# A convolution's output product in pairs of rows: seven half products, sums on GpSimd, the gate kept in DRAM

## The chip, the cores and the metric

The kernel runs on one core of a Trainium2 chip. The metric is the device time of one execution in microseconds (us). The median of three runs of the kernel before is 1639.84 us (1639.81 to 1642.17).

## What is computed

One layer of a backbone with D = 1024 channels, on 128 context tokens and 512 latent tokens, 640 in all, in float32: a gated feed-forward step, a mixer, a second feed-forward step, a final norm. The change lies in the mixer, in the branch of the short convolution and what follows it:

```python
def mixer(h, ...):
    z = h @ w_in + b_in
    ...
    ml = (o * hm) @ w_ml_out
    bg = z[..., B_OFF:C_OFF]
    cg = z[..., C_OFF:X_OFF]
    xs = z[..., X_OFF:GML_OFF]
    u = cg * xs
    ...                                   # uc = centred width-3 convolution of u along the tokens
    sc = (bg * uc) @ w_sc_out             # 1024 x 1024: the product that the change rewrites
    y = jax.nn.sigmoid(z[..., GML_OFF:GSC_OFF]) * ml + jax.nn.sigmoid(z[..., GSC_OFF:IN_COLS]) * sc
    return y @ w_o, C, n, m
...
    mod = jax.nn.silu(cond) @ w_mod + b_mod          # nine vectors of 1024: shifts, scales, gates
    sh1, sc1, g1, shm, scm, gm, sh2, sc2, g2 = jnp.split(mod, N_MOD, axis=-1)
    ...
    x = x + gm[:, None, :] * y
    h = modulate(rmsnorm(x, norm_g[2]), sh2, sc2)
```

## The kernel before, in words

Channels lie on the 128 partitions and tokens along the free axis, so that a row (an output block of 128 channels) is 128 x 640, in two halves of 320 tokens. A float32 product is made of three passes of TensorE (`three`, L288 to L290): weight and activation are each split into a rounded high part and a residual (`split`: ScalarE casts the high part, L75, VectorE subtracts it, L79, named wh/wl for weights, ...h/...l for activations), and hi x hi, hi x lo and lo x hi are added up in PSUM. Each pass is one matmul of 128 x 128 weights on 320 tokens.

A plain row (`plain_el`) is 8 blocks of input channels x 2 halves x 3 passes = 48 matmuls. It consumes two weight operands of 128 x 512, each cast and subtracted once.

A pair (`pair_el`) computes two rows at once. Seen as 2 x 2 blocks (two rows by two halves of the input channels, times two halves of the input channels by two halves of the tokens) it needs seven block products instead of eight, 12 matmuls each, 84 in all, in the order A11, S1, S2, A12, S3, S4, A22. Seven weight operands are split, of which four (S1 to S4) are sums made first (`ws`, L270); S1 and S3 are made on GpSimd where the pair is built with `G`, the rest on VectorE. The activations have seven block operands as well ("11", "21", "22" and the sums "T1" to "T4"). The partial results are moved between PSUM banks by ScalarE (L332, L343, L347) and VectorE: L360 adds the stored S1 product to the bank in which A22 is accumulated next, so A22 waits for L360, and S4's product runs in between. With `spare_v` a ScalarE copy (L357) reads that bank in place of L360. L367 makes the first row's second half. Then `ev` is called for each of the four quarters.

Each engine works through its instructions in the order in which the code emits them. Weight operands are cast four ahead of their use, evictions come after the product that they read, and what `lazy` holds (splits of activations, side terms of the convolution) is emitted in portions between the products. `fill` spreads other steps over the products of an element.

The stages around the change, in the order of the kernel before:
- The convolution's inputs: pairs `cx_pair` (u and its convolution, into the tiles CV) and `bg_pair` (times bg, then split into Bh/Bl), both with sums on GpSimd.
- The gate: four pairs `gsc_pair` (sigmoid, kept in SBUF as GS), sums on VectorE.
- The convolution's output product: eight plain rows over `w_sc_out`; `sc_ev` multiplies by the gate (L2078), adds the other branch's row t, which `t_in` loads back from DRAM (td), halved on the way (L2079), and splits the result into YB.
- The output projection: rows over `w_o`, five plain ones and three in `halves_el`, added into the residual X (L1020), which `x_in` loads back; then the squares for the next norm (L883).
- Modulation vectors: a half of one (512 channels) is computed either on TensorE (`mod_half`: two bursts of four matmuls, L649, and four transposes, L661) or on VectorE (`mod_dve`: 16 instructions of 128 x 512, or 32 of 128 x 256, L767 and L769, then four small matmuls, L778, and two transposes, L786). Three halves are done on VectorE between the rows of `w_sc_out` and `w_o`: both of SC2 and one of G2, in halves of 256 (`h_wide`).

## Time and profile before

| | |
|---|---|
| profiled execution: time | 1639.97 us |
| its span | 1637.9 us |
| TensorE busy | 1616.8 us (99%) |
| VectorE busy | 1308.5 us (80%) |
| ScalarE busy | 883.4 us (54%) |
| GpSimd busy | 318.6 us (19%) |
| convolution's inputs, gate, output product | about 890 to 1037, 1037 to 1083, 1083 to 1140 us of the span |

Times inside the span are counted from its start. A row of a timeline gives start, duration, engine, line, operation, output <- inputs and shape; consecutive instructions overlap a little, so what an instruction costs its engine is the distance from its start to the next one's. A row of a table of windows gives, for a stretch, its length and then each engine's busy time, with the number of instructions in brackets. A row of a table of groups gives the count, the busy time, the mean duration in ns, and the idle time before them.

### The profile page before, as it was taken

Reading aid. Unit: us, or ns where it says so; the run is one execution under the profiler, and the core shown is the slowest. Engines: PE = TensorE matmul, PEld = TensorE weight load, DVE = VectorE, ACT = ScalarE, POOL = GpSimd, SP = SyncE. Lnnn points to the kernel's source line nnn. Section 1 sums busy time; section 2 is a strip of 40 time slices with the busy share of each in tenths; the row PEclk is TensorE's granted clock in tenths of the full one; section 3 lists DMA queues with packets and bytes.
Section 4 is the critical chain, followed back from the end, with each engine's and each line's share of the span. In section 5 each row is a group of like instructions: output and inputs, shape, how many; then the busy total and the mean of one; then the engine's idle time right before and its main releaser. Section 6 shows DMA issues by size and latency. Waiting matters only on the chain.

```text
span 1637.9 us, 29686 instructions
## 1 busy us (share of the span) xinstructions
PE 1616.8 (99%) x10997; PEld 1570.5 (96%) x10997; DVE 1308.5 (80%) x2738; ACT 883.4 (54%) x1957; POOL 318.6 (19%) x441
## 2 busy tenths in 40 slices
PE   8999999999999999999999999999999999999998
PEld 5999999999989999999999999999999999999997
DVE  6878878979777878878887899779688877786765
ACT  5556555655376646555561455533275665565543
POOL 2312311120121322111022222011123113113002
PEclk9999999999999999999999999999999999999999
DMA  9897966785552534333367433357377768468432
GB/s 322 223 228 176 229 134 136 185 224 161 151 180 75 121 90 111 80 94 76 89 215 244 114 91 103 109 174 220 117 187 186 149 133 196 104 137 195 135 114 64
DMA packets 334225, 248.69 MB, mean 152 GB/s; under 512 B 11764, under 2 KB 306043, under 8 KB 334081
## 3 DMA queue, kind: packets, MB, share of 16 engines
q1 hardware_dynamic: 280560, 174.09, 36.8%
q0 software_dynamic: 53488, 72.70, 21.1%
q8 instruction: 86, 1.41, 0.4%
q14 instruction: 59, 0.48, 0.1%
q10 hardware_dynamic: 32, 0.01, 0.0%
HBM read 210.48 MB, written 36.28 MB: 151 GB/s over the span
## 4 chain that ended last, share of the span: by engine, by line
PE 85%; DVE 8%; ACT 3%; issue 1%; DMA 1%; SPq 1%; ACTq 0%; DVEq 0%
PE ps L288 26%; PE ps L289 26%; PE ps L290 26%; DVE wl L79 2%; PE ax L1799 2%; PE ax L1830 2%; DMA wr<-in_ffn_w_dram 1%; PE ax L1802 1%; DVE ws L270 1%; ACT wh L75 1%; PE ax L1776 1%; DVE ma L769 0%; ACT Uh L934 0%; SPq L627 0%; DVE Uh L926 0%
## 5 line engine op out<-in xcount | busy, mean ns | idle before, releaser
L79 DVE TENSOR_TENSOR wl<-wr,wh 128x512 fp32r<-128x512 f32 (+1 forms) x397 | 279.0, 712 | 86.5 <-ACT wh L75 84.4
L79 DVE TENSOR_TENSOR wl<-ws,wh 128x512 fp32r<-128x512 f32 x308 | 211.5, 687 | 62.1 <-ACT wh L75 61.6
L75 ACT CAST wh<-wr 128x512 fp32r<-128x512 f32 (+1 forms) x399 | 235.5, 606 | 35.5 <-PE ps L289 13.4
L75 ACT CAST wh<-ws 128x512 fp32r<-128x512 f32 x308 | 189.2, 620 | 96.8 <-DVE ws L270 86.3
L288 PE MATMUL ps<-HT4h,wh 128*128 128x320 f32 x440 | 138.9, 316 | 1.0 <-DVE t L360 0.9
L288 PE MATMUL ps<-Uh,wh 128*128 128x320 f32 x440 | 137.2, 312 | 0.0
L289 PE MATMUL ps<-HT4l,wh 128*128 128x320 f32 x440 | 136.5, 310 | 0.6 <-DVE HT4l L79 0.5
L289 PE MATMUL ps<-Ul,wh 128*128 128x320 f32 x440 | 136.0, 309 | 0.0
L290 PE MATMUL ps<-HT4h,wl 128*128 128x320 f32 x440 | 136.0, 309 | 0.0
L290 PE MATMUL ps<-Uh,wl 128*128 128x320 f32 x440 | 135.7, 308 | 0.0
L288 PE MATMUL ps<-HT3h,wh 128*128 128x320 f32 x388 | 122.0, 314 | 1.0 <-ACT ps L347 0.8
L289 PE MATMUL ps<-HT3l,wh 128*128 128x320 f32 x388 | 119.9, 309 | 0.0
L290 PE MATMUL ps<-HT3h,wl 128*128 128x320 f32 x388 | 119.9, 309 | 0.0
L288 PE MATMUL ps<-H11h,wh 128*128 128x320 f32 x376 | 119.1, 317 | 0.5 <-ACT H11h L75 0.5
L288 PE MATMUL ps<-H21h,wh 128*128 128x320 f32 x376 | 117.5, 312 | 0.0
L289 PE MATMUL ps<-H11l,wh 128*128 128x320 f32 x376 | 116.5, 310 | 0.7 <-DVE H11l L79 0.4
L290 PE MATMUL ps<-H21h,wl 128*128 128x320 f32 x376 | 116.2, 309 | 0.0
L290 PE MATMUL ps<-H11h,wl 128*128 128x320 f32 x376 | 116.2, 309 | 0.0
L289 PE MATMUL ps<-H21l,wh 128*128 128x320 f32 x376 | 116.0, 309 | 0.0
L235 POOL DMA_DIRECT2D wr<-in_ffn_w_dram x48 | 62.2, 1454 | 275.3 <-DMA wr<-in_ffn_w_dram 121.4
L288 PE MATMUL ps<-H22h,wh 128*128 128x320 f32 x344 | 107.9, 314 | 0.0
L289 PE MATMUL ps<-H22l,wh 128*128 128x320 f32 x344 | 106.5, 310 | 0.4
(489 smaller groups left out, 4929.7 us busy)
## 6 DMA issues: line engine op xcount, KB each, us to landing
wr<-in_ffn_w_dram SPq DMA_DIRECT2D x94, 512.0 KB, 5.8
wr<-in_w_in_dram SPq DMA_DIRECT2D x72, 512.0 KB, 3.9
wr<-in_w_mod_dram SPq DMA_DIRECT2D x59, 512.0 KB, 4.1
xd<-x POOLq DMA_DIRECT2D x56, 320.0 KB, 6.8
wr<-in_ffn_w_dram SPq DMA_DIRECT2D x52, 256.0 KB, 4.4
wr<-in_ffn_w_dram POOLq DMA_DIRECT2D x48, 256.0 KB, 5.3
early<-in_w_mod_dram SPq DMA_DIRECT2D x13, 512.0 KB, 8.8
wq<-in_ffn_w_dram SPq DMA_DIRECT2D x24, 256.0 KB, 3.1
```

What stands on the lines that cost most here:

```text
L75: A.copy(hi, raw)
L79: V.tensor_sub(lo, raw, f32(hi))
L235: queue.dma_start(t[:, 512 * o:512 * o + 512].rearrange("p (k n) -> p k n", k=4), dap(w, (row0 + 512 * half) * ncol + col0, [[ncol, P], [P ...
L270: engine.tensor_add(t, part(o, a), part(o, b))
L288: PE.matmul(ps, hi[:, ws], ah, start=start, stop=False, skip_group_check=True)
L289: PE.matmul(ps, hi[:, ws], al, start=False, stop=False, skip_group_check=True)
L290: PE.matmul(ps, lo[:, ws], ah, start=False, stop=stop, skip_group_check=True)
L1776: PE.matmul(p[:, :P], S["k", dt][:, sl], S["q", dt][:, sl], start=(dt == 0), stop=(dt == 1))
L1799: PE.matmul(p2[:, :DH + 1], S["q", dt][:, sl], S["C"][d][:, dt, :], start=(dt == 0), stop=(dt == 1))
L1802: PE.matmul(p1[:, :DH + 1], S["p", ch][:, d, :], PO["vt"][:, ch, :], start=True, stop=True)
L1830: PE.matmul(p[:, :DH + 1], kw[:, dt * P:(dt + 1) * P], PO["vt"][:, ch, :], start=True, stop=True)
```

## The change

The eight plain rows over `w_sc_out` become four pairs (`sc_pair`). Their seven activation operands per block of input channels are made in `bg_pair` and after it: "11", "T1", "21" and "22" in the B pool (`own`), "T2", "T3" and "T4" in tiles that the layer's input gives free (`lent`). The sums for T1 to T4 are 16 instructions of 128 x 320 on GpSimd. The gate's pairs make their S1 and S3 on GpSimd too; two of them run before the convolution's inputs, two after. Their sigmoids are written to DRAM (sd), and `rows_in` loads gate and other branch back two rows at a time. The halving of the other branch is moved into the constant `HM`, so that the addition (L2098 of the new kernel) is a plain sum, on GpSimd for the second half of the tokens. One half of SC2 is computed on TensorE (`own_units`, in the second and third pair), the other half and G2's on VectorE beside the rows of `w_o`, in one piece of 512. Five rows of `w_o` have the residual of their weights subtracted on GpSimd (`lo=G`).

```diff
+    SO = {o: [None] * 4 for o in OPS_H}
+    LENT = {"T2": "11", "T3": "T1", "T4": "T2"}
...
     def bg_pair(m):
         def ev(mi, h, src):
-            uc = CV[m + mi][:, hsl(h)]
-            V.scalar_tensor_tensor(uc, src, bias(B_OFF + (m + mi) * P), uc, op0=OP.add, op1=OP.mult)
-
-            def put_b():
-                PB[m + mi, h] = bpair()
-                split(uc, *PB[m + mi, h])
-            lazy.append(put_b)
+            r, k = m + mi, (m + mi) % 4
+            c0, c1 = (CV[k][:, hsl(i)] for i in range(2))
+            d0, d1 = (CV[r][:, hsl(i)] for i in range(2))
+            uc = (d0, d1)[h]
+            V.scalar_tensor_tensor(uc, src, bias(B_OFF + r * P), uc, op0=OP.add, op1=OP.mult)
+            if h == 0:
+                lazy.append(own("11" if r < 4 else "21", k, d0))
+            elif r < 4:
+                lazy.extend([lambda: G.tensor_sub(c0, c1, c0), own("T1", k, c0)])
+            else:
+                lazy.extend([own("22", k, d1), lambda: G.tensor_sub(c0, c0, d1), lambda: G.tensor_sub(c1, c1, d1),
+                             lambda: G.tensor_add(d0, d0, c0)])
...
     def gsc_pair(m):
         def ev(mi, h, src):
-            if h == 0:
-                GS[m + mi] = xp.tile([P, T], F32, name="x", bufs=KT)
-            A.activation(GS[m + mi][:, hsl(h)], src, AF.Sigmoid, bias=bias(GSC_OFF + (m + mi) * P))
+            t = t3()
+            A.activation(t, src, AF.Sigmoid, bias=bias(GSC_OFF + (m + mi) * P))
+            G.dma_start(sd[m + mi][:, hsl(h)], t)
...
-    def sc_ev(m):
-        def ev(h, ps):
-            g = GS[m][:, hsl(h)]
-            t = TL[m, h]
-            V.tensor_mul(g, ps, g)
-            V.scalar_tensor_tensor(t, t, 0.5, g, op0=OP.mult, op1=OP.add)
...
+    def rows_in(m):
+        for i in range(m, m + 2):
+            for to, src in ((GS, sd), (TL, td)):
+                to[i] = xp.tile([P, T], F32, name="x", bufs=KT)
+                G.dma_start(to[i], src[i])
...
+    def sc_pair(m):
+        def ev(mi, h, src):
+            r = m + mi
+            g = GS[r][:, hsl(h)]
+            V.tensor_mul(g, src, g)
+            (G if h else V).tensor_add(g, g, TL[r][:, hsl(h)])
...
+    def own_units(pairs, ch, half, p0):
+
+        us, fs = mod_half(ch, half, True)
...
-        conv.append(pair_el(*bg_pair(m), G, spare_v=True))
-    conv += weave([pair_el(*gsc_pair(m)) for m in range(0, KT, 2)], [step(lambda: None)] * 3 + [step(t_in(0))])
-    prog += with_units(conv, mod_dve(SH2, (0,), m_wide), places=[1, 0, 0] * 3 + [1] + [0] * 4)
...
-    sc = [plain_el(w_load(w_sc_out, 0, KT, m * P, D), KT, lambda k, h: PB[k, h], sc_ev(m)) for m in range(KT)]
...
-    prog += with_units(sc + wo, mod_dve(SC2, (0, 1), h_wide) + mod_dve(G2, (1,), h_wide), 2)
+    conv = gs[:2] + cx[:2] + bg[:1] + cx[2:4] + bg[1:2] + cx[4:] + bg[2:] + gs[2:]
+    prog += with_units(conv, mod_dve(SH2, (0,), m_wide), places=[1, 1, 0, 1, 1] + [0] * 9)
...
+    sc = []
     for m in range(0, KT, 2):
...
+        at = {6: [lambda m=m: rows_in(m + 2)]} if m < 6 else {5: [relax, lambda: [x_in(k) for k in range(4)]]}
...
+        sc.append(pair_el(*sc_pair(m), G, acts=SO, at=at))
+    own_units(sc, SC2, 0, 1)
...
+    wo = [dict(el, ops=[dict(o, lo=G) for o in el["ops"]]) for el in wo]
...
+    prog += sc + with_units(wo, mod_dve(SC2, (1,), ma_wide) + g2, places=[2, 2, 1, 2, 1])
```

What VectorE has to do in the output product is other work afterwards. In the kernel before, its instructions for one plain row, from the gate's multiplication of the first half to the last split of a weight, and the first of the modulation's instructions that follow (ps is PSUM, x the gate's tile, t3 the other branch's, wr a loaded weight; the numbers name buffers):

```order
L2078 TENSOR_TENSOR x_13277<-ps_13787,x_13277 128x320
L2079 SCALAR_TENSOR_TENSOR t3_13703<-t3_13703,x_13277 128x320
L2078 TENSOR_TENSOR x_13277<-ps_13788,x_13277 128x320
L2079 SCALAR_TENSOR_TENSOR t3_13705<-t3_13705,x_13277 128x320
L79 TENSOR_TENSOR H11l_13866<-t3_13703,H11h_13865 128x320
L79 TENSOR_TENSOR HT3l_13870<-t3_13705,HT3h_13869 128x320
L79 TENSOR_TENSOR wl_13878<-wr_13857,wh_13877 128x512
L79 TENSOR_TENSOR wl_13882<-wr_13857,wh_13881 128x512
L769 SCALAR_TENSOR_TENSOR HT1h_13713<-wr_13743,cm_93,HT1h_13713 128x256
```

In the changed kernel, VectorE's instructions from the second pair's A12 product on, to the end of that pair:

```order
L2097 TENSOR_TENSOR x_13931<-ps_13939,x_13931 128x320
L2098 TENSOR_TENSOR x_13931<-x_13931,x_13933 128x320
L270 TENSOR_TENSOR ws_14025<-ws_14005,wr_13830 128x512
L79 TENSOR_TENSOR wl_14028<-ws_14005,wh_14027 128x512
L360 TENSOR_TENSOR t3_14043<-ps_14003,t3_13983 128x320
L79 TENSOR_TENSOR H21l_14046<-x_13744,H21h_14045 128x320
L79 TENSOR_TENSOR wl_14059<-ws_14025,wh_14058 128x512
L367 TENSOR_TENSOR t3_13983<-ps_13958,t3_13983 128x320
L2097 TENSOR_TENSOR x_13931<-t3_13983,x_13931 128x320
L79 TENSOR_TENSOR H22l_14078<-x_13744,H22h_14077 128x320
L79 TENSOR_TENSOR H21l_14082<-x_13931,H21h_14081 128x320
L79 TENSOR_TENSOR wl_14088<-wr_13830,wh_14087 128x512
```

The modulation's instructions have gone from here, and sums and splits of weights have come, with L360 in their middle. GpSimd has only loads at this place in the kernel before (t3 from td, x from the residual's xd):

```order
L2091 DMA x_13873<-xd_133 128x640
L2069 DMA t3_13897<-td_174 128x320
L2069 DMA t3_13899<-td_174 128x320
L2091 DMA x_13961<-xd_133 128x640
L2069 DMA t3_13985<-td_174 128x320
```

In the changed kernel it has, from the first pair's end into the second (ws a sum of weights, x the gate's and the other branch's tiles):

```order
L2098 TENSOR_TENSOR x_13740<-x_13740,x_13742 128x320
L270 TENSOR_TENSOR ws_13909<-wr_13469,wr_13615 128x512
L2089 DMA x_13931<-sd_182 128x640
L2089 DMA x_13933<-td_174 128x640
L2089 DMA x_13935<-sd_182 128x640
L2089 DMA x_13937<-td_174 128x640
L2098 TENSOR_TENSOR x_13744<-x_13744,x_13746 128x320
L270 TENSOR_TENSOR ws_14005<-wr_13969 128x512
```

Sums of activations and of weights now share GpSimd's queue with the loads of the next two rows. On TensorE the modulation's four matmuls stand between the S3 and S4 products of the second pair and of the third:

```order
L290 MATMUL ps<-HT1h,wl 128x320
L649 MATMUL ax<-wr,cm 32x512 x4
L288 MATMUL ps<-Bh,wh 128x320
```

They come ahead of S4 there, and so between L360's input and the product A22 that waits for L360.

More of the change, by code (lines that the diff above doesn't have):

```diff
@@ L72, in mixer_step, with split @@
     owed = []
-    def split(raw, hi, lo, owe=False):
+    def split(raw, hi, lo, owe=False, engine=None):
         A.copy(hi, raw)
@@ L78, in split @@
         else:
-            V.tensor_sub(lo, raw, f32(hi))
+            (engine or V).tensor_sub(lo, raw, f32(hi))
     RAWB, HALFB, OPB, SB, AHEAD = 5, 1, 6, 3, 4
@@ L2216, in mixer_step @@
                     {0: (), 1: (3, 2, 1), 2: (2, 2, 2), 3: (3, 2)})
-    els[0][0][0]["fill"] = [step(f) for f in N["later"] + [lambda: None] * 6]
+    els[0][0][0]["fill"] = [step(f) for f in N["later"] + g2_end + [lambda: None] * 6]
+    els[0][0][0]["first"] = []
+    els[0][0][1]["first"] = [lambda: PO["ma_x"].close()]
     els[0][0][-1]["fill"] = [step(half_gate(G2))]
```

80 lines of the change are left out of this document (51 added, 29 removed).

## The prediction

> **What bounds the kernel now.** I read the busy times of the page first, then a table of windows over the stages that the change touches, then TensorE's waits there. In the windows the columns after the length are TensorE, its weight loads, VectorE, ScalarE and GpSimd; then come TensorE's granted clock, the DMA share and GB/s.
>
> ```profile
> PE 1616.8 (99%) x10997; PEld 1570.5 (96%) x10997; DVE 1308.5 (80%) x2738; ACT 883.4 (54%) x1957; POOL 318.6 (19%) x441
> ...
> 890.00:940.00 50.00, 50.00 (x347) 49.38 (x347) 43.64 (x72) 21.25 (x43) 13.52 (x12) 1.00 0.45 130
> 940.00:990.00 50.00, 49.48 (x334) 48.80 (x334) 46.75 (x79) 27.38 (x56) 11.79 (x8) 1.00 0.32 87
> 990.00:1037.00 47.00, 45.84 (x308) 44.89 (x307) 44.43 (x82) 25.09 (x52) 6.02 (x4) 1.00 0.37 100
> 1037.00:1086.00 49.00, 49.00 (x339) 48.39 (x338) 32.18 (x57) 28.66 (x58) 3.25 (x6) 1.00 0.44 127
> 1086.00:1114.00 28.00, 28.00 (x196) 27.39 (x195) 27.26 (x66) 6.71 (x14) 4.77 (x9) 1.00 0.74 222
> 1143.00:1178.00 35.00, 35.00 (x245) 34.38 (x244) 25.86 (x60) 10.70 (x24) 4.96 (x6) 1.00 0.49 145
> ...
> PE ps L288 <- DVE t L360: 0.9, 2, 0.5
> ```
>
> TensorE is the bound everywhere, at full clock: in the output product (1086 to 1114) and the gate (1037 to 1086) it never stops. So a matmul taken away shows in the time, unless another engine takes over. The candidate is VectorE: 44.43 us of 47 in the convolution's inputs, where pairs with sums on GpSimd run as they will in the output product, and there TensorE does lose 0.52 and 1.16 us (50 - 49.48, 47 - 45.84). 0.9 us of that waits for L360, the eviction that must be done before a pair's last product. So VectorE near 95% costs TensorE 1 to 2.5%: what the change is worth hangs on VectorE in the new pairs.
>
> **TensorE: 48 matmuls fewer.** Eight plain rows have 8 x 48 = 384 matmuls, four pairs 4 x 84 = 336. One costs the distance between starts, not its duration of 0.31 us:
>
> ```profile
> 1083.11 0.31 PE L288 MATMUL ps<-Bh,wh 128*128 128x320 f32 x1
> ...
> 1091.03 0.31 PE L288 MATMUL ps<-Bh,wh 128*128 128x320 f32 x1
> ```
>
> These two have 53 matmuls between them: 7.92 / 54 = 0.1467 us. 48 of them are 7.04 us. A pair is 84 x 0.1467 = 12.32 us, a product 1.76 us.
>
> **TensorE: a half of a modulation comes to it.** Two bursts of four matmuls and four transposes; the first feed-forward has the same, here one burst and one set of transposes with their neighbours:
>
> ```profile
> 125.83 0.30 PE L290 MATMUL ps<-HT3h,wl 128*128 128x320 f32 x1
> 126.06 1.06 PE L649 MATMUL ax<-wr,cm 128*32 128x512 f32 x8
> ...
> 127.31 0.31 PE L289 MATMUL ps<-H22l,wh 128*128 128x320 f32 x1
> ...
> 139.34 0.31 PE L290 MATMUL ps<-HT3h,wl 128*128 128x320 f32 x1
> 139.49 0.60 PE L661 MATMUL ax<-ident,t 128*128 128x128 f32 x4
> ...
> 140.08 0.30 PE L289 MATMUL ps<-H22l,wh 128*128 128x320 f32 x1
> ```
>
> The outer rows are two ordinary steps apart (0.29 us) where nothing stands between them. So a burst costs 127.31 - 125.83 - 0.29 = 1.19 us, the transposes 140.08 - 139.34 - 0.29 = 0.45; in all 2 x 1.19 + 0.45 = 2.83 us. What the half cost TensorE while VectorE made it, four small matmuls and two transposes, goes:
>
> ```profile
> 1110.24 0.31 PE L290 MATMUL ps<-Bh,wl 128*128 128x320 f32 x1
> ...
> 1111.30 0.30 PE L289 MATMUL ps<-Bl,wh 128*128 128x320 f32 x1
> ...
> 1118.04 0.31 PE L290 MATMUL ps<-Bh,wl 128*128 128x320 f32 x1
> ...
> 1118.55 0.31 PE L289 MATMUL ps<-Bl,wh 128*128 128x320 f32 x1
> ```
>
> In the same way (1.06 - 0.29) + (0.51 - 0.29) = 0.99 us. Net +1.84 us. The two halves that stay on VectorE cost TensorE what they did. TensorE's own sum is -7.04 + 1.84 = -5.2 us.
>
> **VectorE in the new pairs.** Its price per instruction is again a distance between starts:
>
> ```profile
> 957.53 0.48 DVE L79 TENSOR_TENSOR Bl<-x,Bh 128x320 fp32r<-128x320 f32 x1
> 957.93 0.69 DVE L79 TENSOR_TENSOR wl<-wr,wh 128x512 fp32r<-128x512 f32 x1
> 958.53 0.48 DVE L79 TENSOR_TENSOR Bl<-x,Bh 128x320 fp32r<-128x320 f32 x1
> ```
>
> 0.40 us for 320 columns, 0.60 for 512. By the order, the four pairs hold 31 instructions of 512 and 45 of 320 (seven weight splits, two sums, four products with the gate, two additions, four splits, L360 and L367 a pair, two lent operands extra, and less at the end where GpSimd splits `w_o`): 18.6 + 18.0 = 36.6 us, and I add 2 us for three small ones of the modulation and for instructions that read the result of the one before. On top comes what GpSimd takes from VectorE:
>
> ```profile
> 946.17 0.74 DVE L769 SCALAR_TENSOR_TENSOR x<-wr,cm,x 128x512 f32<-128x512 f32 x1
> ...
> 947.76 1.78 DVE L769 SCALAR_TENSOR_TENSOR x<-wr,cm,x 128x512 f32<-128x512 f32 x1
> ...
> 947.64 1.34 POOL L270 TENSOR_TENSOR ws<-wr 128x512 f32<-128x512 f32 x1 [1.75 <-issue]
> ...
> L79 DVE TENSOR_TENSOR wl<-wr,wh 128x512 fp32r<-128x512 f32 x35 | 31.0, 892 | 5.2 <-ACT wh L75 5.0
> L79 DVE TENSOR_TENSOR wl<-ws,wh 128x512 fp32r<-128x512 f32 x43 | 29.3, 682 | 1.2 <-ACT wh L75 1.2
> L769 DVE SCALAR_TENSOR_TENSOR x<-wr,cm,x 128x512 f32<-128x512 f32 x28 | 23.7, 857 | 0.3
> L1943 DVE SCALAR_TENSOR_TENSOR t<-t,biT,t 128x320 f32<-128x320 f32 x6 | 6.2, 1028 | 0.0
> L2046 DVE SCALAR_TENSOR_TENSOR x<-t,biT,x 128x320 f32<-128x320 f32 x8 | 6.1, 767 | 0.1
> L1943 DVE SCALAR_TENSOR_TENSOR t<-ps,biT,t 128x320 f32<-128x320 f32 x6 | 3.3, 544 | 0.0
> ...
> L270 POOL TENSOR_TENSOR ws<-wr 128x512 f32<-128x512 f32 x20 | 29.2, 1462 | 80.3 <-DVE ws L270 55.2 <-ACT ps L332 13.2 <-issue 8.9
> L883 POOL TENSOR_TENSOR sqacc<-sqacc,t 128x320 f32<-128x320 f32 x10 | 9.9, 1001 | 46.3 <-ACT t L879 46.3
> ```
>
> The same instruction takes 0.74 us alone and 1.78 when a GpSimd sum starts just before it; with an operand in PSUM (t<-ps) nothing is lengthened. Over 877 to 1037 the groups above are longer than their undisturbed like by 35 x 0.210 + 28 x 0.117 + 6 x 0.484 + 8 x 0.223 = 15.3 us, under 20 GpSimd sums: 0.77 us each, about half of a sum's 1.46. A GpSimd sum of 320 has no such count; its bounds are nothing and its whole 1.00 us, and I take 0.7, nearer the top, because each stands among VectorE's own two-operand instructions. In the four pairs GpSimd has about 11 instructions of 512 (7 sums of weights, 4 residuals, priced as sums) and 8 of 320: 8.5 + 5.6 = 14 us. VectorE's need is 36.6 + 2 + 14 = 52.7 us against TensorE's 4 x 12.32 + 2.83 = 52.1. Even. The two bursts stand just ahead of S4 in two pairs, which gives L360 1.19 us more beside S4's 1.76. Weights are ready four products ahead. I take 0.8 us of stalls, bounds 0 and 5: 5 if every extra microsecond of a need of 56 to 57 us (sums at 1.0, additions at 1.0) reaches TensorE.
>
> [...]
>
> **The other parts.**
> - Sums for T1 to T4, 16 on GpSimd, at 0 to 1.00 us of VectorE: 12 fall into the last two `bg` pairs and the gate's pair after them, about eight beside `bg`, 5.6 us. Those pairs evict that bank on ScalarE, and the gate's pair behind them needs far less of VectorE (32.18 us in four). Half of the modulation that shared VectorE with the inputs runs beside the gate now. The 1.7 us that TensorE loses in the inputs could go or double; I take no change, -1.7 to +2.
> - The gate's sums on GpSimd: VectorE has a third of that stage free and gives up two sums a pair. The ten splits lent to the last gate pair, 4 us, fit there; cover gone, they would delay the first new pair by that.
> - The gate through DRAM: 16 writes behind the sigmoid on GpSimd's queue, where the sum for six products later waits behind them; nothing needs it sooner. Reading back is 16 loads of 320 KB, for which a like one shows:
>
> ```profile
> x<-gd POOLq DMA_DIRECT2D x8, 320.0 KB, 4.9
> ```
>
>   They are issued at the end of a pair and first read after the next pair's fourth product, 7 us later. Four at a time make that the second tightest point; I take nothing, at most 2 us a pair.
> - `w_o` with ten residuals on GpSimd: VectorE is rid of 10 x 0.60 = 6 us and loses 10 x 0.77 = 7.7 to the blocks, beside 32 modulation instructions of 512 at 0.66 (946.17 to the next start), 21 us. With the additions to X that is about as long as TensorE's 35.2 us. The first row also needs the last pair's splits within six microseconds. I take 0.5 us, 0 to 2.
> - The constant 0.25, and the last steps of G2 moved into the next feed-forward: same instructions, no change.
>
> **Sum.** -7.04 + 1.84 + 0.8 + 0.5 = -3.9 us. The profiled execution took 1639.97 us (2.1 us around its span of 1637.9), 0.13 above the median of 1639.84, so 1636.1 in that execution and 1635.9 against the median: 0.24% faster. About 0.2%, 3.3 us, is what a measurement of this kernel can tell from no change.
>
> **Rivals.**
> 1. VectorE paces the new pairs and `w_o`: stalls of 2 to 7 us, mostly on L360, give back the gain. For it: VectorE's need equals TensorE's before any idle time of its own, and 95% already cost 1 to 2.5%. Against: the bursts are slack where L360 needs it. Time 1637 to 1642, typically 1638.6 (stalls of 4).
> 2. More is gained than the sum has: no stall in the pairs or `w_o`, and the 1.7 us of the inputs go too. Then -5.2 - 1.7 = -6.9, 1632.9 us. Against: VectorE has no spare time anywhere for it.
> 3. Slower: GpSimd blocks VectorE for the whole of each instruction. Then the pairs need 36.6 + 2 + 11 x 1.46 + 8 x 1.00 = 62.7 us against 52.1; less the 1.8 us that L360 may lag, TensorE waits 8.8. -5.2 + 8.8 + 0.5 = +4.1, 1643.9 us. For it: 947.76. Against: an instruction with a PSUM operand, or a wait, covers part of a block, and 20 sums cost 15.3 us, not 29.2. The sign turns once a GpSimd instruction takes about 83% of its length from VectorE: (52.1 + 1.8 + 4.7 - 38.6) of 24.1 us.
> 4. Slower: the rows come back late. VectorE stands at the gate's product with L360 and the weights behind it; 3 us in each of three pairs make 1645. Against: 4.9 us to land, 7 allowed.
> 5. The saved matmuls bring nothing since the pairs are as long as the rows: that is the first rival at its worst.
>
> **How the numbers follow.** The forecast and the second rival: 0.53 (0.43 and 0.10), with 1633 to 1636.5 between them. The first rival 0.32, of which 0.03 lies beyond 1643. The third 0.10, the fourth 0.05. So faster 0.53, within 0.2% 0.29, slower 0.18. The range runs from the second rival's 1632.9 to 1642.8, which takes in the first rival and leaves out the third and fourth.
>
> **What would show it.** Right: 336 matmuls of the convolution's product in 49 to 50 us plus 2.8 for the modulation; VectorE at 95% or more there with TensorE's waits on L360 below 1 us in sum; weight splits near 0.8 us on average. Wrong: several waits of TensorE on L360 or on wl of over a microsecond; VectorE waiting for loads from sd or td; GpSimd's wl later than `w_o` needs it; or TensorE slower in the inputs than in the kernel before.

## The result, and the profile after

The changed kernel takes 1667.94 us (median; 1667.1 to 1670.14), the kernel before beside it 1639.82: a ratio of 1.0171 (1.0153 to 1.0189), 28 us slower, where 1635.9 was forecast. The profiled execution took 1667.1 us, with a span of 1665.3. The page's busy times of the changed kernel:

```profile
PE 1623.1 (97%) x10959; PEld 1571.3 (94%) x10959; DVE 1332.7 (80%) x2689; ACT 901.2 (54%) x1993; POOL 389.0 (23%) x507
```

No engine has become the bound of the whole: TensorE lost two points, VectorE's share is what it was. The place is found with one row for the convolution's inputs (920 to 1060) and one for gate, output product and w_o (1060 to 1200). Table of windows, changed kernel:

```profile
920.00:1060.00 140.00, 134.41 (x912) 132.44 (x911) 124.32 (x204) 75.60 (x155) 45.29 (x38) 1.00 0.36 100
1060.00:1200.00 140.00, 122.38 (x762) 115.24 (x761) 116.86 (x174) 55.10 (x118) 64.41 (x70) 0.93 0.55 174
```

The same two windows of the kernel before:

```profile
920.00:1060.00 140.00, 138.32 (x937) 136.08 (x936) 124.81 (x215) 78.42 (x161) 24.75 (x19) 1.00 0.36 98
1060.00:1200.00 140.00, 139.84 (x971) 137.44 (x973) 109.56 (x248) 49.94 (x104) 20.52 (x31) 1.00 0.52 155
```

TensorE is idle 5.6 + 17.6 us instead of 1.7 + 0.2, which is 21.4 more. In the second window the granted clock averages 0.93 instead of 1.00: it is 0.50 in four stretches of 20.5 us together, in which TensorE is busy 17.1 us. Matmuls of 320 columns start 0.267 us apart there and 0.147 us apart at 1.00, so I estimate the cost of the slow clock at 17.1 x (1 - 0.147 / 0.267) = 7.7 us. With the 5.2 us that TensorE was to save this makes +23.9 of the +27.4 us between the spans; the rest is not assigned. VectorE is busy 116.86 of the 140 us (83%), but not evenly: 80% in the output product (1080 to 1140), and 19.38 of 20 us from 1160 to 1180, in w_o. TensorE's waits from 880 to 1260 (total, count, longest):

```profile
PE ps L288 <- ACT ps L332: 8.5, 5, 3.1
PE ps L288 <- DVE t L360: 7.8, 6, 2.6
PE ax L778 <- DVE ma L769: 5.1, 2, 4.7
```

These are evictions of PSUM on ScalarE and VectorE, and the reduction of a modulation. In the inputs and in the output product one pattern made them late: an instruction that waits stands at the head of an engine's queue, and work that is ready stands behind it. The longest stall, 4.7 us in w_o, is of another kind: there VectorE works without a break.

### The profile page after: what moved, and what is told of

Its sections match the earlier page's. It is cut to its first block, busy times and chain, and to the rows that moved or that the text cites. A ratio compares the mean times of both kernels' runs of the same rounds, so it can differ in the third digit from the quotient of the medians.

```text
span 1665.3 us, 29744 instructions
## 1 busy us (share of the span) xinstructions
PE 1623.1 (97%) x10959; PEld 1571.3 (94%) x10959; DVE 1332.7 (80%) x2689; ACT 901.2 (54%) x1993; POOL 389.0 (23%) x507
## 3 DMA queue, kind: packets, MB, share of 16 engines
q0 software_dynamic: 54768, 77.95, 21.4%
## 4 chain that ended last, share of the span: by engine, by line
PE 78%; DVE 10%; issue 4%; ACT 4%; DMA 3%; POOL 1%; SPq 0%; ACTq 0%; DVEq 0%; POOLq 0%
PE ps L288 23%; PE ps L289 23%; PE ps L290 23%; DVE wl L79 2%; PE ax L1799 2%; PE ax L1830 2%; DVE ma L769 1%; DVE ws L270 1%; PE ax L1802 1%; DMA wr<-in_ffn_w_dram 1%; DMA wr<-in_w_sc_out_dram 1%; ACT wh L75 1%; POOL ws L270 1%; DMA early<-in_w_mod_dram 1%; PE ax L1776 1%
## 5 line engine op out<-in xcount | busy, mean ns | idle before, releaser
L79 DVE TENSOR_TENSOR wl<-ws,wh 128x512 fp32r<-128x512 f32 x324 | 228.0, 704 | 61.0 <-ACT wh L75 60.3
L75 ACT CAST wh<-ws 128x512 fp32r<-128x512 f32 x324 | 200.1, 622 | 128.4 <-DVE ws L270 83.8
L288 PE MATMUL ps<-H22h,wh 128*128 128x320 f32 x376 | 118.5, 315 | 0.0
L289 PE MATMUL ps<-H22l,wh 128*128 128x320 f32 x376 | 116.8, 311 | 0.4
L290 PE MATMUL ps<-H22h,wl 128*128 128x320 f32 x376 | 116.6, 310 | 0.0
L288 PE MATMUL ps<-H11h,wh 128*128 128x320 f32 x360 | 114.1, 317 | 1.6 <-ACT ps L332 1.1
L289 PE MATMUL ps<-H11l,wh 128*128 128x320 f32 x360 | 111.6, 310 | 0.7 <-DVE H11l L79 0.4
```

The costliest lines, as they stand in the source:

```text
L75: A.copy(hi, raw)
L79: (engine or V).tensor_sub(lo, raw, f32(hi))
L288: PE.matmul(ps, hi[:, ws], ah, start=start, stop=False, skip_group_check=True)
L289: PE.matmul(ps, hi[:, ws], al, start=False, stop=False, skip_group_check=True)
L290: PE.matmul(ps, lo[:, ws], ah, start=False, stop=stop, skip_group_check=True)
```

## The experiments

All times are medians; ratios are against the kernel before, run beside them. Each of the first nine is the changed kernel (1667.94, 1.0171) with one edit. Runs of one such kernel lie 1.4 to 5.4 us apart. Clear of that are the gains of the first three rows; SC2's half earlier and bursts of two lie at its edge, and the other four can't be told from the changed kernel.

| kernel | us | ratio (95%) |
|---|---|---|
| output product's arithmetic on VectorE | 1659.57 | 1.0114 (1.0097 to 1.0131) |
| only its additions on VectorE | 1659.47 | 1.0122 (1.0105 to 1.0139) |
| sums for T on VectorE | 1660.49 | 1.0129 (1.0114 to 1.0144) |
| T1's cast later | 1666.61 | 1.0168 (1.0154 to 1.0182) |
| SC2's half on TensorE earlier | 1663.78 | 1.0148 (1.0133 to 1.0163) |
| the same half spread over four pairs | 1668.49 | 1.0180 (1.0165 to 1.0196) |
| w_o residuals on VectorE | 1669.92 | 1.0185 (1.0170 to 1.0200) |
| w_o modulation on TensorE, bursts of two | 1664.12 | 1.0150 (1.0135 to 1.0165) |
| the same, bursts of four | 1670.37 | 1.0187 (1.0171 to 1.0202) |
| kernel before with pauses | 1655.29 | 1.0097 (1.0079 to 1.0116) |
| repairs together, first | 1650.87 | 1.0072 (1.0057 to 1.0087) |
| second | 1652.94 | 1.0084 (1.0070 to 1.0098) |
| third | 1648.17 | 1.0047 (1.0034 to 1.0061) |
| fourth | 1645.97 | 1.0043 (1.0031 to 1.0056) |
| fifth | 1642.33 | 1.0019 (1.0010 to 1.0028) |
| sixth | 1637.77 | 0.9989 (0.9980 to 0.9997) |
| seventh | 1638.08 | 0.9994 (0.9985 to 1.0003) |

**The output product: additions on GpSimd (8.5 us).** All of that stage's arithmetic taken off GpSimd, and then its additions alone:

```diff
-            (G if h else V).tensor_add(g, g, TL[r][:, hsl(h)])
+            V.tensor_add(g, g, TL[r][:, hsl(h)])
```

The first of the two runs also has

```diff
-        sc.append(pair_el(*sc_pair(m), G, acts=SO, at=at))
+        sc.append(pair_el(*sc_pair(m), acts=SO, at=at))
```

> In the output product no arithmetic is left on GpSimd: S1 and S3 and all additions of the other branch are on VectorE. Theory V with a heavy block (VectorE is held up by GpSimd for most of each instruction): VectorE takes on 8 x 0.60 + 8 x 0.40 = 8 us and is rid of up to 8 x 1.46 + 8 x 1.0 = 19.7 us, so the stalls on L360 in the output product go: 1660 to 1663. Theory G: the sums no longer wait in GpSimd's queue, which gains as well: 1661 to 1664. Theory R: the late weights still hold up the sums, now on VectorE, where L360 stands behind them: 1667 to 1672.

> Only the additions of the other branch (L2098, eight of 128x320) are moved from GpSimd to VectorE; the sums for the weights stay on GpSimd. Theory G (an addition waits up to 6.9 us for VectorE's product with the gate, and the weight sum queued behind it on GpSimd waits with it): most of the 8 us that the run with all arithmetic of that stage on VectorE gained: 1660 to 1663. Rival (it is the sums' own 1.46 us and their blocks of VectorE that count): 1665 to 1668, VectorE has 3.2 us more to do.

Measured 1659.57 and 1659.47, both just below what was expected of the queue (1661 to 1664, then 1660 to 1663); the rival of the second run, 1665 to 1668, is out. The eight additions are the whole effect, and moving the weight sums too adds nothing that can be measured. Rows of timelines of the changed kernel (in brackets the idle time before, and its releaser):

```profile
1105.21 9.16 SPq L218 DMA_DIRECT2D wr<-in_w_sc_out_dram  x2
...
1110.14 1.06 POOL L2098 TENSOR_TENSOR x<-x 128x320 f32<-128x320 f32 x1 [6.91 <-DVE x L2097]
1111.16 1.74 POOL L270 TENSOR_TENSOR ws<-wr 128x512 f32<-128x512 f32 x1
1112.84 0.56 POOL L2089 DMA_DIRECT2D x<-sd  x1
...
1120.86 1.29 POOL L270 TENSOR_TENSOR ws<-wr 128x512 f32<-128x512 f32 x1 [3.74 <-DMA wr<-in_w_sc_out_dram]
...
1122.18 0.62 ACT L75 CAST wh<-ws 128x512 fp32r<-128x512 f32 x1 [5.16 <-POOL ws L270]
...
1122.18 0.69 DVE L270 TENSOR_TENSOR ws<-ws,wr 128x512 f32<-128x512 f32 x1 [2.98 <-POOL ws L270]
...
1123.98 0.41 PE L288 MATMUL ps<-HT2h,wh 128*128 128x320 f32 x1 [1.48 <-DVE t L360]
```

GpSimd stands 6.91 us at an addition that waits for VectorE's product with the gate. Behind it stand the sum S3 and the four loads that bring the rows back. These then go out from 1112.84 on, the last at 1114.45, just as the second of the two weight loads in the first line is issued (1105.21 + 9.16 is the end of the two issues, each 0.37 long, so at 1114.0), and that weight lands only at 1120.86. The sum S1 waits for it, ScalarE's cast waits 5.16 us and VectorE's S2 2.98 us for the sum, L360 stands in VectorE's queue behind S2, and TensorE stops. The same place with the additions on VectorE:

```profile
1105.60 8.33 SPq L218 DMA_DIRECT2D wr<-in_w_sc_out_dram  x2
...
1103.61 1.40 POOL L270 TENSOR_TENSOR ws<-wr 128x512 f32<-128x512 f32 x1 [1.09 <-issue]
1104.97 0.56 POOL L2089 DMA_DIRECT2D x<-sd  x1
...
1117.67 2.99 POOL L270 TENSOR_TENSOR ws<-wr 128x512 f32<-128x512 f32 x2 [10.55 <-DMA wr<-in_w_sc_out_dram]
```

The sum and the row loads go out 8 us earlier. The second weight, issued at about 1113.6, lands after 4.1 us instead of 6.9 (one load in each run), and TensorE's stalls of 1.48 and 2.63 us in the next two pairs are 0 and 0.35; one ahead of them, at the first pair, grew from 1.10 to 2.62. Two smaller ones in w_o (0.56 and 1.00) go as well, the 4.7 us there stay, and the clock is slow for 13.7 us instead of 20.5. VectorE's busy time fell from 1332.7 to 1329.3 us although it made eight additions more, so what they took from it by running beside it went as well and is not priced apart; but in the first run eight longer sums left GpSimd too, VectorE's busy time fell from 1329.3 to 1328.2 us although it made them, and the time stayed.

**The convolution's inputs: sums for T on GpSimd (7.4 us).** First the 16 sums on VectorE, then instead only ScalarE's cast one quarter later:

```diff
-                lazy.extend([lambda: G.tensor_sub(c0, c1, c0), own("T1", k, c0)])
+                lazy.extend([lambda: V.tensor_sub(c0, c1, c0), own("T1", k, c0)])
```

with L2071 and L2072 in the same way. In the second run the next `ev` puts into `lazy` what stands in PEND:

```diff
-                lazy.extend([lambda: G.tensor_sub(c0, c1, c0), own("T1", k, c0)])
+                lazy.append(lambda: G.tensor_sub(c0, c1, c0))
+                PEND.append(own("T1", k, c0))
```

> The 16 sums for T1 to T4 are on VectorE instead of GpSimd. Theory G (GpSimd's in-order queue: a sum that waits for VectorE's split of the operand before it holds the weight sums behind it, and ScalarE's cast of T1 that waits for that sum holds the evictions): ScalarE's waits on x L2069 and TensorE's stalls at 970-980, 1010-1020 and 1050-1070 (2.6, 0.7 and 4.1 us) go, with about 1.6 us of slow clock: 1659 to 1662 us. Theory V (VectorE's own load is the limit in the inputs): 16 x 0.40 = 6.4 us more on VectorE, stalls stay or grow: 1667 to 1672.

> The changed kernel, where ScalarE's cast of T1 is emitted one evicted quarter later than GpSimd's sum that it reads; the sum stays on GpSimd. Theory G in its in-order form (ScalarE stands at the cast of T1 and the eviction L332 behind it waits): ScalarE's waits on x L2069 and TensorE's stalls at 970-980 and 1010-1020 (2.6 and 0.7 us) go, the stalls after 1040 stay: 1662 to 1665. Rival (GpSimd's sums cost by blocking VectorE, or VectorE is late anyway): 1666 to 1669.

Measured 1660.49 and 1666.61. The stall of 2.64 us in the changed kernel, followed through four engines:

```profile
972.07 0.49 DVE L79 TENSOR_TENSOR Bl<-x,Bh 128x320 fp32r<-128x320 f32 x1
...
972.63 1.25 POOL L2069 TENSOR_TENSOR x<-x 128x320 f32<-128x320 f32 x1 [11.16 <-DVE Bl L79]
973.84 1.26 POOL L270 TENSOR_TENSOR ws<-wr 128x512 f32<-128x512 f32 x1
...
973.91 0.46 ACT L75 CAST Bh<-x 128x320 fp32r<-128x320 f32 x1 [3.67 <-POOL x L2069]
...
975.66 0.42 ACT L332 COPY ps<-ps 128x320 f32<-128x320 f32 x1
...
976.13 0.41 PE L288 MATMUL ps<-HT2h,wh 128*128 128x320 f32 x1 [2.64 <-ACT ps L332]
```

The sum must wait for VectorE's split of the operand that it overwrites (11.16 us at the head of GpSimd's queue, with the weight sum behind it). ScalarE's cast of T1 must wait for the sum (3.67 us), and L332 is queued behind that cast. VectorE was busy all along until 973.1. TensorE's busy time in 960 to 980 (first number after the length), in the changed kernel, then with the sums on VectorE, then with the later cast:

```profile
960.00:980.00 20.00, 17.36 (x118) 17.11 (x118) 18.68 (x34) 9.68 (x21) 5.57 (x4) 1.00 0.38 106
```

```profile
960.00:980.00 20.00, 18.22 (x123) 17.69 (x122) 19.89 (x33) 10.46 (x22) 5.16 (x4) 1.00 0.42 110
```

```profile
960.00:980.00 20.00, 19.53 (x134) 19.27 (x133) 19.93 (x32) 10.59 (x23) 8.35 (x5) 1.00 0.38 106
```

The later cast frees ScalarE and mends this place better than moving the sums does, so the chain is right here. But the whole run gains 1.3 us, which is within the noise and in the range of its rival: GpSimd still stands at the sums, a wait of 3.1 us on L332 after 1060 remains, and in 1080 to 1100 TensorE is busy 15.19 us where it was 17.77. Moving the sums gains although VectorE is busier at this place, 19.89 of 20 us, so its load isn't the limit here. It does not show that the queue alone cost the 7.4 us: over the whole execution VectorE is busy 1333.0 us with the 16 sums (6.4 us at the prediction's price) and 1332.7 without them, so I estimate that about 6 us by which GpSimd had lengthened its instructions went away with the sums. How much is queue and how much is that stays open.

**The weight ring.** The loads for SC2 taken away from the output product, or spread over its pairs:

```diff
-    own_units(sc, SC2, 0, 1)
+    own_units(own_el, SC2, 0, 0)
```

where `own_el` is the last two gate pairs and the first of sc. In the other run each pair has one load and one burst of two matmuls:

```diff
-    own_units(sc, SC2, 0, 1)
+    sc_end = own_spread(sc, SC2, 0)
+    wo[0] = dict(wo[0], calm=False, first=[open_u2], fill=sc_end)
```

> The half of SC2 on TensorE stands in the last two gate pairs instead of the second and third pair of the output product, so that no modulation load takes a place among the five raw weight buffers there. Theory R (raw buffers: late w_sc_out weights hold up GpSimd's sum, ScalarE's cast behind it and the evictions behind that): weights of the output pairs land within 5 us of their issue instead of 9.2 to 9.5, ScalarE's idle time on ws between 1085 and 1145 falls from 15 us or more to under 4, TensorE gains the 4 to 5 us of stalls there and 1.5 to 3 us of slow clock: 1660 to 1662 us. Theory G (GpSimd's own queue is what is late, whatever the loads): 1666 to 1668.

> The half of SC2 on TensorE is spread over all four pairs of the output product, one load and two matmuls in each, instead of two loads and four matmuls in two pairs; everything else as in the changed kernel. By the order of the five raw buffers a pair's second weight then no longer waits for the first weight of the pair before. Theory R: ScalarE's idle time on ws from 1080 to 1150 falls from 25 us to under 12 and TensorE's idle time there by 3 to 5 us, with one or two fewer drops of the clock: 1661 to 1664. Theory G (GpSimd's additions and sums behind one another are late even when the weights are there): 1665 to 1668.

Measured 1663.78, between its two ranges, and 1668.49, just above its second. In the latter, TensorE's busy time from 1080 to 1140 rose from 53.2 to 56.6 us, so late weights did cost some 3 us there, but an edit of its own lost it again: the three finishing steps stood close together in the first row of w_o, and TensorE waited 8.8 us at the transposes (L661) for a copy queued behind VectorE's splits. The ring is at most a part of the loss: what it costs alone is not shown.

**w_o: a reduction in order (a stall of 4.7 us and the clock behind it).** Residuals back to VectorE; then SC2's other half on TensorE, in bursts of two and of four:

```diff
-    wo = [dict(el, ops=[dict(o, lo=G) for o in el["ops"]]) for el in wo]
```

The second run has one load in each of four rows, the third two loads in each of two:

```diff
-    prog += sc + with_units(wo, mod_dve(SC2, (1,), ma_wide) + g2, places=[2, 2, 1, 2, 1])
+    wo_end = own_spread(wo, SC2, 1)
+    prog += sc + with_units(wo[:4] + [dict(wo[4], fill=wo_end)], g2, places=[1, 1, 1, 1, 0])
```

```diff
+    own_units(wo, SC2, 1, 0)
+    prog += sc + with_units(wo, g2, places=[0, 0, 1, 2, 1])
```

> The ten residuals of the w_o weights are on VectorE again. Theory W (GpSimd's residuals slow VectorE's modulation, and TensorE waits in order at the reduction, L778): the 4.7 us wait on L778 falls below 1 us, and the low clock behind it (0.80 and 0.69 in 1170 to 1190) goes with it: 1659 to 1663. Rival (VectorE simply has too much in that stage: 10 x 0.60 us come back to it, 10 x 0.77 us of blocks go): the wait at L778 stays above 3 us, 1666 to 1669.

> The other half of SC2 is on TensorE as well, one load in each of four rows of w_o, and VectorE makes only the half of G2 there, one load a row; the residuals of the w_o weights stay on GpSimd. Theory W2 (VectorE gets 32 modulation instructions into five rows in a lumped order and TensorE waits in order at the reduction): the waits on L778 go (5 us), the slow clock from 1170 to 1190 goes (about 3 us), TensorE pays 2.83 - 1.0 = 1.84 us: 1660 to 1663. Rival (late w_o weights are the cause, and a third load a row keeps them late): 1666 to 1670.

> The changed kernel with one edit: the second half of SC2 on TensorE in two bursts of four in the first two rows of w_o, and VectorE's half of G2 in the three rows after. Theory W2 (too much modulation for VectorE in the first rows of w_o, TensorE waits in order at the reduction): the 5 us on L778 and 3 us of slow clock go for 1.84 us more work on TensorE, and the run with bursts of two paid 2.4 us more for the same: 1660 to 1662.5. Rival (the burst size costs nothing): 1664, as the run with bursts of two.

Measured 1669.92, 1664.12 and 1670.37: the first and the third lie above both of their ranges, the second between its two. In the changed kernel:

```profile
1170.68 9.68 DVE L769 SCALAR_TENSOR_TENSOR ma<-wr,cm,ma 128x512 f32<-128x512 f32 x8
...
1171.86 6.49 POOL L79 TENSOR_TENSOR wl<-wr,wh 128x512 fp32r<-128x512 f32 x4 [8.43 <-ACT wh L75]
...
1178.96 1.07 PE L778 MATMUL ax<-ma,ones 128*32 128x256 f32 x4 [4.72 <-DVE ma L769]
```

VectorE never stops here. The reduction stands at a fixed place in TensorE's order, and the modulation that it reads isn't finished; a stall of 4.5 to 4.7 us is here in the runs with the additions or the sums for T moved as well, so it doesn't hang on what those edits mend. With the residuals on VectorE the same eight instructions take 5.88 us instead of 9.68:

```profile
1176.63 5.88 DVE L769 SCALAR_TENSOR_TENSOR ma<-wr,cm,ma 128x512 f32<-128x512 f32 x8
```

So four residuals on GpSimd took 3.8 us from VectorE in their 6.49, and by these rows most of the stall of 4.72 us is theirs; about 0.9 us is what I estimate would be left if nothing else moved. Something else did: VectorE made four residuals itself and stood 1.1 and 2.7 us at those of late weights, with the modulation behind them, and the wait on L778 grew to 8.1 us. The run trades a slowed VectorE for a waiting one, and doesn't show either to be the cause alone. With the half on TensorE the waits on L778 are gone, but in the third run TensorE waits 7.2 us at its transposes for a copy on ScalarE, queued behind casts of late weights: another queue, a like stall.

**The clock.** Whether idle time slows the clock, tested in the kernel before, where TensorE doesn't wait in the rows of w_ml_out from the second on:

```diff
+    def pause(m, n):
+        def f():
+            t = t3()
+            G.tensor_copy(t, GM_T[m - 1][:, HT:])
+            for _ in range(n - 1):
+                G.tensor_copy(t, t)
+            PE.transpose(aux()[:, :P], t[:, :P], ident)
+        return step(f)
+    for m, n in ((1, 1), (3, 2), (5, 3), (7, 5)):
+        ml[m]["fill"] = [pause(m, n)] + ml[m]["fill"]
```

> The kernel before, with four pauses of TensorE in the rows of w_ml_out, where it never waits: in the second, fourth, sixth and eighth row a transpose waits for 1, 2, 3 and 5 copies of 128x320 that GpSimd makes one after the other once the row before is evicted. Theory C (after an idle time of about 2 us or more TensorE runs at half clock for some 3 us, which costs about 1.6 us beyond the idle time): the matmuls after the two or three longer pauses start 0.27 us apart instead of 0.147 for a few us, those after the shortest do not; the time is 1639 plus the sum of the pauses plus 1.6 for each slow stretch. Rival (the low clock in the changed kernel has another cause than idle time): all matmuls stay 0.147 apart, and the time grows by the pauses alone.

Measured 1655.29. The four pauses, which do not follow the number of copies, and a window of 2 us behind the first of them:

```profile
859.58 0.33 PE L2123 MATMUL ax<-ident,t 128*128 128x128 f32 x1 [2.60 <-POOL t L2120]
...
877.00 0.33 PE L2123 MATMUL ax<-ident,t 128*128 128x128 f32 x1 [1.45 <-POOL t L2122]
...
893.25 0.33 PE L2123 MATMUL ax<-ident,t 128*128 128x128 f32 x1 [1.07 <-POOL t L2122]
...
913.23 0.48 PE L2123 MATMUL ax<-ident,t 128*128 128x128 f32 x1 [5.35 <-POOL t L2122]
```

```profile
862.00:864.00 2.00, 2.00 (x9) 2.00 (x9) 0.32 (x1) 0.59 (x1) 0.00 (x0) 0.50 0.82 285
```

After 2.60 and 5.35 us of idle time the clock is halved; after 1.45 and 1.07 it stays at 1.00. The halved stretch lasts 5.5 us after the longest pause, 21 matmuls 0.267 us apart: 2.5 us lost. After the 2.60 the clock is 0.74, 0.50 and 0.91 in three windows of 2 us, which is 3.4 us at 0.50: by the same distances I estimate 1.5 lost. Pauses 10.5, slow clock 4.0 and four transposes of 0.1 to 0.3 make about 15 to 16 of the 16.2 us. Idle times of 2.60 and 5.35 us do slow the clock here; the rival is out.

The changed kernel's trace shows more. Its half clock begins at 1070.20, 1094.10, 1141.88 and 1176.02 and lasts 3.41, 3.41, 3.41 and 10.24 us, and the beginnings lie 23.90, 47.78 and 34.14 us apart, which is 7, 14 and 10 times 3.413. I read this as a grid of such stretches through the execution, with the idle time within one of them deciding on the next. The stall of 2.64 us lies across a border, with 1.14 us of idle time in one stretch and 1.50 in the next. Its like in the run with only the additions moved, 2.66 us, lies within one. Both stretches of the changed kernel, then that run's stretch and the one behind it, with the granted clock behind the five busy times:

```profile
971.22:974.63 3.41, 2.27 (x16) 2.02 (x14) 2.16 (x5) 0.46 (x1) 2.00 (x2) 1.00 0.00 1
974.63:978.04 3.41, 1.91 (x13) 1.91 (x14) 3.41 (x5) 2.41 (x5) 2.10 (x2) 1.00 0.12 28
```

```profile
972.42:975.83 3.41, 0.75 (x6) 0.49 (x5) 2.16 (x4) 1.80 (x4) 2.33 (x3) 1.00 0.00 0
975.83:979.24 3.41, 3.41 (x15) 3.41 (x14) 2.81 (x5) 1.60 (x5) 1.27 (x1) 0.50 0.59 154
```

Like stalls were followed by 3.41 us at 0.50 in one run, about 1.5 us of cost by the distances above, and by nothing in the other, and the border fell differently in them.

**Together.** The first combination has the sums for T and the output product's arithmetic on VectorE, SC2's halves on TensorE in bursts of two in the four pairs and in w_o. The next ones change what its trace showed, one or two places at a time. Second: SC2's finishing steps apart, the half of SH2 beside w_ml_out. Third: only two of that half's four loads there, two in the first gate pairs. Fourth: both halves of SC2 in bursts of four, in the last gate pairs and the first rows of w_o. Fifth: both copies of `mod_half`'s sums on VectorE. Sixth: the sixth row's residuals of w_o on GpSimd as well. Seventh: G2's loads one row earlier. The edits of the third, fourth, fifth and sixth in their lines:

```diff
+    prog += with_units(ml, all_[:10], places=[1, 1, 2, 1, 2, 1, 2, 0])
```

```diff
+    own_units(own_el, SC2, 0, 0)
+    own_units(wo, SC2, 1, 0)
```

```diff
-                (A.copy if i else V.tensor_copy)(r[:, :2 * P], S["p"][:, 2 * P * i:2 * P * (i + 1)])
+                (A.copy if i and not on else V.tensor_copy)(r[:, :2 * P], S["p"][:, 2 * P * i:2 * P * (i + 1)])
```

```diff
+    prog.append(dict(last, ops=[dict(o, lo=G) if i < 2 else o for i, o in enumerate(last["ops"])]))
```

> All four together: sums for T1 to T4, sums of weights and additions of the output product on VectorE; SC2's first half spread over four pairs and its second half on TensorE. If the causes are separate their gains add: 7.4 (sums for T) + 8.4 (output product's arithmetic) + 5 to 8 (w_o) less 1 or 2 for what is shared with the raw buffers: 1644 to 1650. If VectorE becomes the bound (it takes 6.4 + 8 us more in stages that were at 90 to 95%): 1650 to 1656. If nothing stalls any more, what is left is the saving of 7.04 less 2 x 1.84 for the two halves on TensorE: 1636 to 1638.

> The combination, with two more edits: the last three steps of SC2's first half (copy, transposes, reduction) stand apart over the second row of w_o instead of close together in the first, where TensorE waited 3.6 us for the copy; and the half of SH2 that VectorE makes beside the convolution's inputs is made beside the rows of w_ml_out, where VectorE is at 75%. If the wait for the copy and VectorE's load in the inputs are what was left, 3.6 us, the slow clock behind it (1 to 1.6) and 3 to 4 of the 5 us of waits in the inputs go: 1641 to 1643. If nothing stalls more than in the kernel before: 1636 to 1638. Rival: with the modulation the rows of w_ml_out stall, or the inputs stay as they are: 1646 to 1651.

> As the run before with the moved half of SH2, but only two of its four loads stand beside the rows of w_ml_out, none in the last of them, and the other two in the first two gate pairs, where the changed kernel has two as well. That run lost 7.7 us and the slow clock behind it (0.83 of a 20-us window, 3.4 us) at one place, the end of the w_ml_out rows, where VectorE stood at a sum of weights that were loaded late, with the additions that free PSUM behind it. If that was all that the move cost: 1641 to 1643 us. If the inputs, the gate, the output product and w_o then stall no more than 3 us in all, against 1.7 in the kernel before: 1637 to 1639, as fast as the kernel before or faster by what TensorE saves (7.04 - 2 x 1.84 = 3.4 us). Rival (the late weights come back at another place): 1644 to 1652.

> The combination once more, with both halves of SC2 on TensorE in bursts of four matmuls instead of two: the first half in the last two gate pairs, the second in the first two rows of w_o, the half of G2 in the three rows after; SH2 as in the run before, but with its reductions one a row. In the run before four bursts of two cost TensorE 1.2 us each, what a burst of four costs in the kernel before (99.43 - 97.94 - 0.29 = 1.20 at 1098), so that each half cost 4 x 1.2 + 0.45 = 5.25 us and not 2.83. If that is what was left over (2 x 2.4 = 4.8 us), with 3.9 us of waits on L778 in the w_ml_out rows: 1638 to 1641. If the bursts of two are not the cause: 1643 to 1649.

> As the run with bursts of four, but both copies of the sums of SC2 out of PSUM are on VectorE (in the run before one stood on ScalarE behind two casts of w_o weights that waited 6.6 us for their load, and TensorE waited 6.5 us in order at the transposes; behind that came a stretch at 0.84 of the clock, 3.2 us in 20). VectorE is busy 4 of 20 us there. If this wait is what was left: 1646.0 - 6.5 - 3 = 1636 to 1638, which is the kernel before less the 3.4 us that TensorE saves, plus one or two of stalls. Rival (the late load stalls TensorE elsewhere in w_o): 1641 to 1646.

> As the run before (1642.3), with one edit: the two weight residuals of the sixth row of w_o are on GpSimd too. In the run before VectorE stood 7.9 us at the first of them, behind ScalarE's cast, which waited for a late load; eight modulation instructions and the additions that free PSUM were queued behind, and TensorE waited 2.4 us for L1020 and ran at 0.85 of the clock after it. If that is right, VectorE makes the modulation while the load is on its way, the wait on L1020 goes: 1637 to 1640, no slower than the kernel before. Rival (the late weight itself is then what TensorE waits for): 1641 to 1645.

> As the other run of this call, with the four loads of G2's half one row earlier (0, 1, 2, 1, 0 over the five rows instead of 0, 0, 1, 2, 1), where VectorE is busy 1.6 of 10 us: none of them stands ahead of the last rows' weights among the five raw buffers. If late weights are all that is left in w_o: 1636.5 to 1638.5, 0.05 to 0.15% under the kernel before. Rival (six modulation loads in the first two rows make the weights of the third late): 1640 to 1646.

The first came to 1650.87, above the range for separate causes and at the lower end of the one in which VectorE becomes the bound. The second, 1652.94, missed all its ranges: it lost 7.7 us at the end of the w_ml_out rows. The third took that away, but it came only to 1648.17, in the range of its rival: 3.9 us went to waits on L778 in the w_ml_out rows, and the rest into something that had looked like no cost. A burst of two matmuls with its neighbours, in the third combination:

```profile
1097.94 0.31 PE L290 MATMUL ps<-HT1h,wl 128*128 128x320 f32 x1
1098.18 1.05 PE L649 MATMUL ax<-wr,cm 128*32 128x512 f32 x4
1099.16 0.42 PE L288 MATMUL ps<-Bh,wh 128*128 128x320 f32 x1
1099.43 0.31 PE L289 MATMUL ps<-Bl,wh 128*128 128x320 f32 x1
```

It costs 1.20 us, as much as the burst of four in the prediction (1.19), so four bursts of two make a half of SC2 dearer by 2.4 us. The fourth repaired that, but at 1645.97 it is again in its rival's range, since it met the wait on ScalarE's queue:

```profile
1160.17 1.14 ACT L75 CAST wh<-wr 128x512 fp32r<-128x512 f32 x2 [6.62 <-DMA wr<-in_w_o_dram]
1161.22 0.36 ACT L656 COPY t<-ax 128x256 f32<-128x256 f32 x1
...
1161.63 0.69 PE L661 MATMUL ax<-ident,t 128*128 128x128 f32 x2 [6.47 <-ACT t L656]
```

The fifth moved the copy to VectorE and came to 1642.33, once more where its rival was, since now a residual of the next late weight stood ahead of other work there:

```profile
1168.38 1.29 DVE L79 TENSOR_TENSOR wl<-wr,wh 128x512 fp32r<-128x512 f32 x2 [7.88 <-ACT wh L75]
1169.59 5.88 DVE L769 SCALAR_TENSOR_TENSOR ma<-wr,cm,ma 128x512 f32<-128x512 f32 x8
...
1176.21 0.39 PE L288 MATMUL ps<-H21h,wh 128*128 128x320 f32 x1 [2.42 <-DVE x L1020]
```

The sixth put that residual on GpSimd's queue, where little stands behind it, and is at 1637.77 in its range and the fastest, 0.9989 (0.9980 to 0.9997). The seventh, in its range too, makes no further difference, and its interval takes in 1.0: the whole loss is gone, and the change pays a little at most. The sixth's windows:

```profile
920.00:1060.00 140.00, 139.45 (x954) 138.51 (x954) 128.83 (x215) 77.49 (x160) 37.44 (x30) 1.00 0.35 96
1060.00:1200.00 140.00, 138.34 (x945) 131.49 (x944) 114.34 (x220) 66.91 (x143) 48.79 (x58) 1.00 0.62 187
```

TensorE is idle 2.2 us there, at full clock.

## Why the prediction was wrong

The forecast added up work per engine and took small sums for stalls. What the changed kernel's profile has in their place (idle time of TensorE beyond that of the kernel before, or the single stalls):

| term | taken, us | measured, us |
|---|---|---|
| stalls in the convolution's inputs | 0 (-1.7 to +2) | 3.9, and 3.1 in the gate pair behind them |
| splits lent to the last gate pair | "fit there" | 1.9 |
| stalls in the new pairs | 0.8 (0 to 5) | 1.10 + 1.48 + 2.63 = 5.2 |
| stalls in `w_o` | 0.5 (0 to 2) | 0.56 + 1.00 + 4.72 + 0.39 = 6.7 |
| slow clock | no term | about 7.7 (estimate) |

**The failed step is "VectorE in the new pairs",** with its likes in the inputs and in `w_o`. The prediction set VectorE's need against TensorE's, found them even, and took 0.8 us of stalls, with "Weights are ready four products ahead" as cover. 5.2 us came, though VectorE was busy only 80% there, not 95%. What came late in the pairs were sums of weights, and a lead of four products is no slack: a cast emitted ahead stands in ScalarE's queue ahead of an eviction, and a late sum stops both. The first pair in the changed kernel:

```profile
1100.70 0.62 ACT L75 CAST wh<-ws 128x512 fp32r<-128x512 f32 x1 [3.08 <-POOL ws L270]
1101.23 0.42 ACT L332 COPY ps<-ps 128x320 f32<-128x320 f32 x1
...
1101.70 0.41 PE L288 MATMUL ps<-H11h,wh 128*128 128x320 f32 x1 [1.10 <-ACT ps L332]
```

That VectorE's load is not what held TensorE up in the pairs shows in the output product of the changed kernel and of the sixth combination (TensorE 53.22 and 59.12 of 60 us, VectorE 48.23 and 56.09):

```profile
1080.00:1140.00 60.00, 53.22 (x342) 49.32 (x340) 48.23 (x73) 29.10 (x65) 27.53 (x33) 0.97 0.59 185
```

```profile
1080.00:1140.00 60.00, 59.12 (x403) 57.55 (x402) 56.09 (x111) 32.47 (x69) 18.99 (x28) 1.00 0.70 216
```

With VectorE busy 93% TensorE loses 0.9 us, once operands come in time. So the first rival had the sign right, waits on L360 of more than a microsecond, but not the reason. The other steps:

- **TensorE's sum** is borne out by the sixth combination. It pays for two halves of SC2, so -7.04 + 2 x 1.84 = -3.4 us by the prediction's prices. From 840 to 1260 its TensorE is idle 4.0 us against 2.3 before. -3.4 + 1.7 = -1.7; measured -1.5, with an uncertainty of about 1.4.
- **Additions on GpSimd** were priced as work that VectorE is rid of, and as blocks. That they wait for VectorE, up to 6.9 us, with the weight sums and the row loads behind them, was not asked; it was worth 8.5 us with the clock.
- **Sums for T:** "I take no change, -1.7 to +2" counted the same way; they were worth 7.4, of which the share of the queue is open.
- **The lent splits** did not fit into the last gate pair: VectorE was busy without a break from 1085.2 on, L360 came late, and TensorE waited 1.93 us.
- **The gate through DRAM:** rows weren't late for VectorE (no wait for sd or td appears), so the fourth rival is out. Queued late, their loads went out together with a weight's load, which took 6.9 us to land and not 4.1. "Nothing needs it sooner" was said of the writes; for the loads the harm lay in their time.
- **w_o, "I take 0.5 us, 0 to 2":** VectorE's time was compared with TensorE's over the whole of the rows. The step left out that the reduction stands in TensorE's order at a fixed place, with eight modulation instructions and GpSimd's residuals just ahead of it.
- **No term for the clock.** About 7.7 of the 28 us, by the estimate above, are work at a clock of 0.50 behind idle times of 1.93 us or more. In a kernel whose TensorE waits 0.7 us at most in these stages, the profile before could not show it.
- **The third rival,** GpSimd blocking VectorE, is real in `w_o` (3.8 us of 6.49, just ahead of the longest stall) and not refuted in the inputs. In the output product it is not what cost the time: with the additions gone, taking the weight sums off GpSimd too changed nothing. The 3.8 of 6.49 us in `w_o` are 59%; no run here shows the whole of GpSimd's instructions on average.

What stays open: how the places share the slow clock, since each stall that goes shifts the others; the single gains (8.5 for the additions, 7.4 for the sums for T, 4.2 for SC2's half earlier) don't add up to the whole, perhaps for that reason.

## What to carry to other kernels

Before a step is moved to an engine with time to spare, write down what stands behind it in that engine's queue and what it waits for there: a short instruction that waits long (here an addition of 1.06 us, 6.91 us) costs everything behind it, and a lead in the order (here four products) is no slack on a queue that also evicts. Ask also what an instruction that another engine needs at a fixed place has just ahead of it. Where TensorE sets the time, price a stall of two microseconds or more with the slow clock that can follow it (here 3.41 us at 0.50 behind one of 1.93 us), and look at the next queue as soon as one is mended.
